# Two-layer encoder trunk on one core: weight sums and every second low part of the up weights by adding DMAs, down-projection operands made one block earlier

## The chip, the cores and the metric

The kernel runs on one core of a Trainium2 chip. The metric is the device time of one execution in microseconds (us). The kernel before was run three times; one further execution was profiled, and all rows below come from that one.

## The reference

Two layers; in each a mixer (layer 0: latent attention and stick-breaking attention side by side; layer 1: forgetting attention), a layer norm, a SwiGLU feed-forward block, a second layer norm, and a gated embedding. Everything is float32, with SEQ = 512, D_MODEL = 1024, D_FF = 2816. The change touches the feed-forward block and the loading of weights for it and for the gate:

```python
def swiglu(x, w1, w3, w2):
    return (jax.nn.silu(x @ w1) * (x @ w3)) @ w2

    for i in range(DEPTH):
        j = i // 2
        ...
        x = layer_norm(DEEPNORM_ALPHA * x + mix, ln1_g[i], ln1_b[i])
        x = layer_norm(DEEPNORM_ALPHA * x + swiglu(x, ffn_w1[i], ffn_w3[i], ffn_w2[i]), ln2_g[i], ln2_b[i])
        x = x + jax.nn.sigmoid(x @ ple_w_gate[i] + ple_b_gate[i]) * (p[i] @ ple_w_proj[i])
```

## The kernel before

Float32 products are made of three matmuls on rounded parts: each operand is split into a high part, rounded to TensorE's short float32 format, and a low part, the rest; `mm3` (L151 to L154) issues high x low, high x high and low x high. The activations stand in SBUF as x transposed, `xTh` and `xTl`. Weights come in chunks of 128 x 512 through `wload` (L138 to L149): SyncE loads `wraw` (256 KB, three buffers), ScalarE rounds it to `whi` (L147), and a subtraction makes `wlo` (L148). Which engine subtracts is told by a table; in the feed-forward block it is `DENSE`, in turn DVE, DVE, GpSimd (POOL in the profile). High and low parts have four buffers of 128 x 1024 each.

`swiglu` (L652) works on 22 blocks f of 128 hidden columns. `up` (L656) loads the pieces of w1 and w3 for one block, makes 48 matmuls into `ps_h`, and writes the gated product. The first 16 blocks are taken in four groups of four. For each group `down` (L694) makes the down-projection as seven products in place of eight (a Strassen-like scheme over halves of the hidden columns and of the output columns): `operands(m)` builds product m's activation side `bparts` (L734, L735) and its weight side, which is a block of w2 (`w2raw`, loaded as 1024 KB pieces) or a sum of such blocks, `s3` or `s1`, made by DVE and GpSimd (L713); ScalarE rounds it (L740), and DVE and GpSimd take one half each of the low part (L741). A product is 12 matmuls into `ps_m`, 84 per group. `down` is a generator, and its steps are woven into the next group's blocks, two after each `up`; `operands(m + 1)` is made ahead of product m's matmuls. The six blocks that are left (plain) follow: in the first pair of them the last group's steps are run (three, three and one), then `flush` (L767) adds up the products, and `down_pair` (L780) makes the plain blocks' own down-projection in `ps_y`. The last pair goes to `finish`, which also makes the second layer norm and the gate (L610 to L649), tile by tile of 128 rows: the statistics on ScalarE (L194), the normalising steps on DVE (L195, L199) and GpSimd (L196 to L201), the transposes of x on TensorE (`ps_xt`, L177), the gate's matmuls (`ps_g`).

The order in which instructions stand on an engine is set by a scheduler with estimates of its own, from this program order and the waits between instructions; each engine then runs its list in order. POOL's list holds GpSimd's instructions and the DMAs that GpSimd issues; all loads of weights are issued by SyncE.

## Time and profile before

| | us |
|---|---|
| three runs | 1392.1, 1392.12, 1394.07 (median 1392.12) |
| the profiled execution | 1396.08 |
| its span, first to last instruction | 1394.4 |
| mean granted TensorE clock | 0.986 of full speed |
| TensorE (PE) busy | 1346.4 (97%) |
| VectorE (DVE) busy | 925.9 (66%) |
| ScalarE (ACT) busy | 659.9 (47%) |
| GpSimd (POOL) busy | 534.1 (38%) |

The span is 1.7 us less than the execution's time; the rest lies before the first and behind the last instruction. In the rows below, L148 is line 148 of the kernel before, names are the program's tiles, out<-in, and a row of a window or group gives busy time and a count of instructions. PEclk is the granted clock as a share of full speed. "idle before, <-releaser" is the time for which an engine stood still ahead of the instruction, and the instruction that it waited for.

### The profile page before, as it was taken

To read this page: it belongs to the slowest core of one execution; us is meant where nothing else is said; L and a number is where in the kernel's file an instruction comes from. 1 tells how busy PE (TensorE), PEld (TensorE's weight loads), DVE (VectorE), ACT (ScalarE), POOL (GpSimd) and SP (SyncE) were. 2 spreads that over 40 slices of the span, in tenths; PEclk is the share of its full clock that TensorE was granted. 3 is DMA by queue.
4 is the path that set the end of the run, shared out by engine and by line. 5 is a ranking of instruction groups with operands and counts; after the bars stand their busy time and mean duration, and the time that the engine had idled before them with its cause. 6 is when DMAs were issued, how large, how long until landed. Compare 5 with 4: busy or idle time off the path is not lost.

```text
span 1394.4 us, 18865 instructions
## 1 busy us (share of the span) xinstructions
PE 1346.4 (97%) x6680; PEld 1126.1 (81%) x6680; DVE 925.9 (66%) x1600; ACT 659.9 (47%) x1362; POOL 534.1 (38%) x479
## 2 busy tenths in 40 slices
PE   7999999799999998999989999998999999989998
PEld 7888787588888887887879888876888888868887
DVE  4656778753757656948755775798346668578495
ACT  4556767552433333423455665754434334243252
POOL 5655733122334324612235554442224334255131
PEclk9999999999999999999999999999999999999999
DMA  6211321241323132232234221123413131403312
GB/s 230 89 44 47 112 66 62 90 159 61 121 83 102 58 115 89 101 105 75 73 111 131 98 91 62 61 99 105 143 56 135 54 121 44 167 32 129 98 61 98
DMA packets 64303, 131.74 MB, mean 94 GB/s; under 512 B 7361, under 2 KB 8129, under 8 KB 64193
## 3 DMA queue, kind: packets, MB, share of 16 engines
q1 hardware_dynamic: 61440, 120.74, 25.6%
q0 software_dynamic: 2768, 9.80, 2.1%
q8 instruction: 52, 0.85, 0.3%
q14 instruction: 43, 0.34, 0.1%
HBM read 127.80 MB, written 2.72 MB: 94 GB/s over the span
## 4 chain that ended last, share of the span: by engine, by line
PE 84%; DVE 9%; ACT 3%; DMA 2%; issue 2%; POOL 0%; SPq 0%; DVEq 0%; ACTq 0%; POOLq 0%
PE ps_h L154 11%; PE ps_h L153 11%; PE ps_h L152 11%; PE ps_m L152 4%; PE ps_m L153 4%; PE ps_m L154 4%; PE ps_qkT L152 3%; PE ps_qkT L153 3%; PE ps_qkT L154 3%; PE ps_y L152 2%; PE ps_o L406 2%; PE ps_y L153 2%; PE ps_y L154 2%; PE ps_g L152 2%; PE ps_g L154 2%; PE ps_g L153 2%
## 5 line engine op out<-in xcount | busy, mean ns | idle before, releaser
L148 POOL TENSOR_TENSOR wlo<-wraw,whi 128x512 fp32r<-128x512 f32 (+2 forms) x191 | 255.3, 1346 | 453.5 <-ACT whi L147 402.3
L147 ACT CAST whi<-wraw 128x512 fp32r<-128x512 f32 (+1 forms) x338 | 200.1, 616 | 323.3 <-DMA wraw<-in_ffn_w_dram 83.6
L152 PE MATMUL ps_h<-xTl,whi 128*128 128x512 f32 (+1 forms) x736 | 279.8, 380 | 0.0
L153 PE MATMUL ps_h<-xTh,whi 128*128 128x512 f32 (+1 forms) x736 | 279.6, 380 | 0.0
L154 PE MATMUL ps_h<-xTh,wlo 128*128 128x512 f32 (+1 forms) x736 | 279.5, 380 | 0.0
L148 DVE TENSOR_TENSOR wlo<-wraw,whi 128x512 fp32r<-128x512 f32 (+1 forms) x172 | 141.9, 837 | 92.9 <-ACT whi L147 90.5
L153 PEld LDWEIGHTS ps_h<-xTh,whi 128*128 128x128 f32 x736 | 138.4, 188 | 26.5
L152 PEld LDWEIGHTS ps_h<-xTl,whi 128*128 128x128 f32 x736 | 138.4, 188 | 26.2
L154 PEld LDWEIGHTS ps_h<-xTh,wlo 128*128 128x128 f32 x736 | 138.4, 188 | 26.1
L152 PE MATMUL ps_m<-wlo,bparts 128*128 128x512 f32 x224 | 89.4, 399 | 9.4 <-DVE wlo L741 8.9
L153 PE MATMUL ps_m<-whi,bparts 128*128 128x512 f32 x224 | 88.8, 396 | 0.0
L154 PE MATMUL ps_m<-whi,bparts 128*128 128x512 f32 x224 | 88.5, 395 | 0.0
L152 PE MATMUL ps_qkT<-xTl,whi 128*128 128x512 f32 x192 | 78.5, 409 | 2.4 <-DVE qkT L331 1.0
L154 PE MATMUL ps_qkT<-xTh,wlo 128*128 128x512 f32 x192 | 78.0, 406 | 0.0
L153 PE MATMUL ps_qkT<-xTh,whi 128*128 128x512 f32 x192 | 77.5, 404 | 0.0
L740 ACT CAST whi<-s 128x512 fp32r<-128x512 f32 x64 | 36.9, 619 | 85.4 <-PE ps_h L153 49.6
L741 POOL TENSOR_TENSOR wlo<-s,whi 128x512 fp32r<-128x512 f32 x32 | 42.8, 1340 | 76.3 <-ACT whi L740 76.3
L741 POOL TENSOR_TENSOR wlo<-w2raw,whi 128x512 fp32r<-128x512 f32 x24 | 34.6, 1440 | 91.9 <-ACT whi L740 83.3
L152 PE MATMUL ps_v<-wlo,xTh 128*128 128x256 f32 (+1 forms) x192 | 56.3, 294 | 6.8 <-ACT neg_tri L109 6.4
L682 DVE TENSOR_TENSOR gb<-silu,ps_h 128x256 f32<-128x256 f32 x64 | 24.0, 416 | 57.5 <-PE ps_h L154 53.7
L152 PEld LDWEIGHTS ps_m<-wlo,bparts 128*128 128x128 f32 x224 | 42.9, 192 | 20.0 <-DVE wlo L741 9.7
L210 DVE TENSOR_TENSOR x<-x,ps_y 128x512 f32<-128x512 f32 x64 | 43.0, 679 | 22.9 <-PE ps_y L154 22.6
(274 smaller groups left out, 3216.1 us busy)
## 6 DMA issues: line engine op xcount, KB each, us to landing
wraw<-in_ffn_w_dram SPq DMA_DIRECT2D x200, 256.0 KB, 2.7
w2raw<-in_ffn_w_dram SPq DMA_DIRECT2D x16, 1024.0 KB, 6.4
wraw<-in_w_gate_dram SPq DMA_DIRECT2D x32, 256.0 KB, 2.6
wraw<-in_w_qkf_dram SPq DMA_DIRECT2D x32, 256.0 KB, 2.6
wraw<-in_w_qkb_dram SPq DMA_DIRECT2D x16, 256.0 KB, 2.9
wraw<-in_a_w_out_dram SPq DMA_DIRECT2D x16, 256.0 KB, 2.6
kbias<-nd_dram POOLq DMA_DIRECT2D x8, 512.0 KB, 4.8
wraw<-in_c_w_out_dram SPq DMA_DIRECT2D x16, 256.0 KB, 2.6
```

The costliest lines, as they stand in the source:

```text
L147: (eng_hi.copy if eng_hi is acts else eng_hi.tensor_copy)(hi[:, c:end], raw)
L148: eng_lo.tensor_tensor(lo[:, c:end], raw, hi[:, c:end].bitcast(F32), ALU.subtract)
L152: nc.tensor.matmul(o, lhsT=lhs[0], rhs=rhs[1], start=first, stop=False)
L153: nc.tensor.matmul(o, lhsT=lhs[0], rhs=rhs[0], start=False, stop=False)
L154: nc.tensor.matmul(o, lhsT=lhs[1], rhs=rhs[0], start=False, stop=last)
L210: nc.vector.tensor_tensor(xs, xs, ps, ALU.add)
L406: nc.tensor.matmul(o_ps[:, kb * P:], lhsT=val[:, c:c + 2 * HD], rhs=t, start=first and n == 0, stop=last and n == 1, skip_group_check=True)
L682: nc.vector.tensor_tensor(half[:, p, k, :], s[:, fs], h[:, fs], ALU.mult)
L740: acts.copy(wh[q], ws[q])
L741: (dve, gps)[(q + m) % 2].tensor_tensor(wl[q], ws[q], wh[q].bitcast(F32), ALU.subtract)
```

## The change

Four things are changed.

**Every second low part by ScalarE and a DMA.** `SWIGLU` is the table for the weights of the feed-forward blocks, of the plain blocks' rows of w2 and of the gate's first half. One chunk in two has its low part subtracted by DVE. For the other ScalarE writes the chunk's negative into the place of `wlo`, which rounds it as the high part is rounded, and a DMA issued by GpSimd adds the chunk to it from memory once more. These are 108 chunks: 44 of w1, 44 of w3, 12 of w2's plain rows and 8 of the gate. GpSimd makes no low part of these weights any more.

**Weight sums by DMA.** `s3` and `s1` are no longer added by DVE and GpSimd from `w2raw`. Each is written by one DMA of 512 KB from w2 and then added to by another, `add` in `down`; later steps add two more blocks to `s1`. These are 48 DMAs, 16 that write and 32 that add, on GpSimd's queue. One quarter of w2 is then no longer loaded to `w2raw`. All low parts of the products' weights (L741 before) are made by DVE.

**Operands ahead.** `operands(0)` of a group is made when `down` is first entered, right behind the group's fourth block, and not with the first product's matmuls. The order of the first two products is swapped, and so are the indices of the halves.

**The plain blocks.** The last group's seven products are spread two per block over the first plain blocks, `flush` comes after the fourth of them, and both `down_pair`s of the first four stand behind the last two blocks.

The number of TensorE's matmuls, their shapes and what is computed stay as they were. The core of the diff:

```diff
...
     STICK = (acts, dve), (gps,)
     MLA = (acts, dve), (gps,)
     FOX = (acts,), (gps,)
+    SWIGLU = (acts,), (dve, nc.sync)
     engines, count = [DENSE], [0]
 
     def wload(src, n, m):
...
             count[0] += 1
             eng_hi, eng_lo = (v[count[0] % len(v)] for v in engines[0])
             (eng_hi.copy if eng_hi is acts else eng_hi.tensor_copy)(hi[:, c:end], raw)
-            eng_lo.tensor_tensor(lo[:, c:end], raw, hi[:, c:end].bitcast(F32), ALU.subtract)
+            if eng_lo is nc.sync:
+                nc.scalar.mul(lo[:, c:end], raw, -1.0)
+                gps.dma_start(lo[:, c:end], src[:, c:end], accum_op=ALU.add)
+            else:
+                eng_lo.tensor_tensor(lo[:, c:end], raw, hi[:, c:end].bitcast(F32), ALU.subtract)
         return [t[:, 0:n * m].rearrange("p (n m) -> p n m", n=n) for t in (hi, lo)]
 
     def mm3(o, lhs, rhs, first, last):
...
 
     def swiglu(i, finish):
         w1, w3, w2 = a["ffn_w1"][i], a["ffn_w3"][i], a["ffn_w2"][i]
+        engines[0] = SWIGLU
         nf = DFF // P
 
         def up(f, g, cuts=1):
...
 
 
             first = f0 == 0
+            blocks = w2[f0 * P:(f0 + 4) * P, :].rearrange("(k q p) (j c) -> p q k j c", q=2, k=2, j=2)
             raw = []
             for p in range(2):
                 t = quad("w2raw", F32)
-                nc.sync.dma_start(t.rearrange("p (k j) c -> p k (j c)", k=2),
-                                  w2[(f0 + 2 * p) * P:(f0 + 2 * p + 2) * P, :].rearrange("(k p) c -> p k c", k=2))
+                nc.sync.dma_start(t[:, 0, :], blocks[:, p, 0, 0, :])
+                nc.sync.dma_start(t[:, 2:4, :], blocks[:, p, 1])
                 raw.append(t)
             B = [[halves[i][:, :, k, :] for i in range(2)] for k in range(2)]
 
             def W(j, k):
                 return [t[:, 2 * k + j, :] for t in raw]
 
-            s3, s1 = ([wide(n)[:, q * S:(q + 1) * S] for q in range(2)] for n in ("s3", "s1"))
+            wsum = [wide(n)[:, 0:D].rearrange("p (q c) -> p q c", q=2) for n in ("s3", "s1")]
+            s3, s1 = ([t[:, q, :] for q in range(2)] for t in wsum)
+
+            def add(t, k, j, first=False):
+                gps.dma_start(t, blocks[:, :, k, j, :], accum_op=ALU.bypass if first else ALU.add)
+
+            add(wsum[0], 0, 0, True)
+            add(wsum[0], 0, 1)
+            add(wsum[1], 0, 1, True)
+            add(wsum[1], 1, 1)
             n1, n2, n3, n4 = (temp(n).rearrange("p (q s) -> p q s", q=2) for n in ("n1", "n2", "n3", "n4"))
-
-            def add(o, a, b, eng):
-                for q in range(2):
-                    eng[q].tensor_tensor(o[q], a[q], b[q], ALU.add)
 
             def operands(m):
                 tt = dve.tensor_tensor
-                ws, bs = [(W(0, 1), B[1][0]), (W(0, 0), B[0][0]), (s3, n3), (s1, n1), (s1, n2), (W(1, 1), n4),
+                ws, bs = [(W(0, 0), B[0][0]), (W(0, 1), B[1][0]), (s3, n3), (s1, n1), (s1, n2), (W(1, 1), n4),
                           (s1, B[1][1])][m]
                 if m == 2:
-                    add(s3, W(0, 0), W(1, 0), (dve, gps))
                     tt(n3, B[0][1], B[1][1], ALU.subtract)
                 elif m == 3:
-                    add(s1, W(1, 0), W(1, 1), (dve, gps))
                     tt(n1, B[0][0], B[0][1], ALU.subtract)
                 elif m == 4:
-                    add(s1, s1, W(0, 0), (dve, gps))
                     dve.scalar_tensor_tensor(n2, B[1][1], -1.0, n1, ALU.mult, ALU.subtract)
                 elif m == 5:
                     tt(n4, n2, B[1][0], ALU.add)
-                elif m == 6:
-                    add(s1, s1, W(0, 1), (dve, gps))
                 parts = act.tile([P, 2, S], F32R, tag="g", bufs=3, name="bparts")
                 bh, bl = (parts[:, c, :].rearrange("p (q s) -> p q s", q=2) for c in range(2))
                 acts.copy(bh, bs)
...
                 wh, wl = ([v[:, q * S:(q + 1) * S] for q in range(2)] for v in (hi, lo))
                 for q in range(2):
                     acts.copy(wh[q], ws[q])
-                    (dve, gps)[(q + m) % 2].tensor_tensor(wl[q], ws[q], wh[q].bitcast(F32), ALU.subtract)
+                    dve.tensor_tensor(wl[q], ws[q], wh[q].bitcast(F32), ALU.subtract)
+                if m == 3:
+                    add(wsum[1], 0, 0)
+                elif m == 4:
+                    add(wsum[1], 1, 0)
                 return (bh, bl), (wh, wl)
 
             ready = operands(0)
+            yield
             for m in range(7):
                 (bs, ws), ready = ready, operands(m + 1) if m < 6 else None
                 for tb in range(2):
                     ps = (ps_pq, ps_o)[tb]("ps_m")
                     for q in range(2):
                         mm3(ps, both(bs, lambda v: v[:, q, blk(tb)]), both(ws, lambda v: v[q]), q == 0, q == 1)
-                    if m in (0, 5, 6):
+                    if m in (1, 5, 6):
                         o = x[tb + 2 * (m == 6)][:, (m == 5) * S:(m == 5) * S + S]
                         if first:
                             dve.scalar_tensor_tensor(o, o, ALPHA, ps, ALU.mult, ALU.add)
...
 
         def flush():
 
-            q1, q7, p5, p6 = (sums[m] for m in (1, 2, 3, 4))
+            q1, q7, p5, p6 = (sums[m] for m in (0, 2, 3, 4))
             h00, h01, h10, h11 = (x_rows[:, 2 * i:2 * i + 2, j * S:(j + 1) * S] for j in range(2) for i in range(2))
             dve.tensor_tensor(p6, q1, p6, ALU.add)
             gps.tensor_tensor(h00, h00, q1, ALU.add)
...
         for f0 in range(0, 4 * GROUPS, 4):
             halves = [spare("gb").rearrange("p (q k s) -> p q k s", q=2, k=2) for _ in range(2)]
             for n in range(4):
-                up(f0 + n, as_block(halves, n // 2, n % 2), 2 if f0 + n == 0 else 1)
+                up(f0 + n, as_block(halves, n % 2, n // 2), 2 if f0 + n == 0 else 1)
                 after_up(2)
             after_up(7)
             steps = down(f0, halves)
-        waiting = None
-        for f in range(nf - plain, nf, 2):
-            group = quad("gT")
-            gs = [(group[:, 2 * j, :], group[:, 2 * j + 1, :]) for j in range(2)]
-            for j in range(2):
-                up(f + j, as_parts(gs[j]))
-                if f == nf - plain:
-                    after_up(3)
-            if waiting is None:
+            next(steps)
+        waiting = []
+        for f in range(nf - plain, nf):
+            if len(waiting) < 2:
+                g = spare("gT", F32R).rearrange("p (c s) -> p c s", c=2)
+            elif f % 2 == 0:
+                group = quad("gT")
+            if len(waiting) >= 2:
+                g = group[:, 2 * (f % 2):2 * (f % 2) + 2]
+            up(f, as_parts((g[:, 0, :], g[:, 1, :])))
+            waiting.append((g[:, 0, :], g[:, 1, :]))
+            after_up(2)
+            if f == nf - plain + 3:
                 after_up(7)
                 flush()
-            else:
-                down_pair(*waiting)
-            waiting = (f, gs)
+            if f >= nf - 2:
+                n = 2 * (f - nf + 2)
+                down_pair(nf - plain + n, waiting[n:n + 2])
+        gs = waiting[-2:]
         finish(gs, row_weights(w2, [nf - 2, nf - 1]))
 
 
...
 
         def finish(gs, w):
             first_half, rest = gate(i, e, a["w_gate"][i], done)
+            engines[0] = DENSE
             finish_rows(gs, w, False, norm_params("ln2_g", "ln2_b"), after=first_half)
             rest()
```

How the change moves instructions is shown at three places. The lines of the changed kernel are its own, five more than before from L152 on (L148 is L153, L741 is L748, L713's sums are the DMAs of L719).

POOL, layer 0, from the first group's products on: the stream of GpSimd. Before (`s_3752`, `s_3753`, `s_3754` are the weight sums of group one):

```order
L713 TENSOR_TENSOR s_3752<-w2raw 128x512
L148 TENSOR_TENSOR wlo<-wraw,whi 128x512 x5
L741 TENSOR_TENSOR wlo<-w2raw,whi 128x512 x2
L741 TENSOR_TENSOR wlo<-s_3752,whi 128x512
L713 TENSOR_TENSOR s_3754<-w2raw 128x512
L148 TENSOR_TENSOR wlo<-wraw,whi 128x512
L741 TENSOR_TENSOR wlo<-s_3753,whi 128x512
L713 TENSOR_TENSOR s_3754<-s_3754,w2raw 128x512
L741 TENSOR_TENSOR wlo<-s_3754,whi 128x512
L713 TENSOR_TENSOR s_3754<-s_3754,w2raw 128x512
L148 TENSOR_TENSOR wlo<-wraw,whi 128x512 x2
L741 TENSOR_TENSOR wlo<-w2raw,whi 128x512
```

In the changed kernel (`s_4192`, `s_4193`, `s_4695` and their like are the same sums, each DMA row one that writes and one that adds, or two that add):

```order
L151 DMA wlo<-in_ffn_w_dram 128x512 x8
L719 DMA s_4192<-in_ffn_w_dram 128x2x512 x2
L151 DMA wlo<-in_ffn_w_dram 128x512 x2
L719 DMA s_3686<-in_ffn_w_dram 128x2x512 x2
L151 DMA wlo<-in_ffn_w_dram 128x512 x2
L719 DMA s_4193<-in_ffn_w_dram 128x2x512 x2
L151 DMA wlo<-in_ffn_w_dram 128x512 x4
L719 DMA s_4695<-in_ffn_w_dram 128x2x512 x2
L151 DMA wlo<-in_ffn_w_dram 128x512 x2
L719 DMA s_4193<-in_ffn_w_dram 128x2x512 x2
```

Sums and subtractions have become DMAs, and in the steady part nothing but DMAs stands on POOL; the two DMAs of a sum stand directly ahead of the two lows of a block, and behind one another.

DVE, layer 0, at the last group: the lows of its products and what stands between them. `gT<-silu` ends a plain block. Before:

```order
L673 TENSOR_TENSOR silu<-silu,ps_h 128x512
L125 TENSOR_TENSOR gT<-silu,gT 128x512
L713 TENSOR_TENSOR s_5246<-w2raw 128x512
L741 TENSOR_TENSOR wlo<-w2raw,whi 128x512
L741 TENSOR_TENSOR wlo<-s_5246,whi 128x512
L713 TENSOR_TENSOR s_5248<-w2raw 128x512
L741 TENSOR_TENSOR wlo<-w2raw,whi 128x512
L713 TENSOR_TENSOR s_5248<-s_5248,w2raw 128x512
L764 TENSOR_TENSOR acc<-acc,ps_m 128x512 x2
L756 TENSOR_TENSOR x<-x,ps_m 128x512
```

In the changed kernel:

```order
L748 TENSOR_TENSOR wlo<-w2raw,whi 128x512 x2
L732 TENSOR_TENSOR n_5206<-gb 128x512
L748 TENSOR_TENSOR wlo<-s_5198,whi 128x512 x2
L742 TENSOR_TENSOR bparts<-n_5206,bparts 128x512
L679 TENSOR_TENSOR silu<-silu,ps_h 128x512
L153 TENSOR_TENSOR wlo<-wraw,whi 128x512
L776 TENSOR_TENSOR acc<-acc,ps_m 128x512
L125 TENSOR_TENSOR gT<-silu,gT 128x512
L776 TENSOR_TENSOR acc<-acc,ps_m 128x512
L153 TENSOR_TENSOR wlo<-wraw,whi 128x512
L768 TENSOR_TENSOR x<-x,ps_m 128x512 x2
L748 TENSOR_TENSOR wlo<-s_5199,whi 128x512 x2
```

Before, the lows of the first products come behind the first plain block's end, with sums between them. Now the first three products' lows stand ahead of that block's end, and the lows of the fourth behind it.

PE, layer 0, second layer norm: the last matmuls of the plain blocks (`ps_y`) and the first transposes of x (`ps_xt`), with buffer numbers. Before:

```order
L153 MATMUL ps_y_5979<-whi_5921,gT_5525 128x512
L154 MATMUL ps_y_5979<-whi_5921,gT_5525 128x512
L177 MATMUL ps_xt_6185<-identr_69,x_78 128x128 x4
L177 MATMUL ps_xt_6192<-identr_69,x_78 128x128 x4
L152 MATMUL ps_y_5987<-wlo_5912,gT_5525 128x512
L153 MATMUL ps_y_5987<-whi_5911,gT_5525 128x512
L154 MATMUL ps_y_5987<-whi_5911,gT_5525 128x512
```

In the changed kernel:

```order
L158 MATMUL ps_y_6180<-whi_6047,gT_5709 128x512
L159 MATMUL ps_y_6180<-whi_6047,gT_5709 128x512
L182 MATMUL ps_xt_6232<-identr_69,x_78 128x128 x4
L182 MATMUL ps_xt_6239<-identr_69,x_78 128x128 x4
L157 MATMUL ps_g_6246<-wlo_6061,xTh_76 128x512
L158 MATMUL ps_g_6246<-whi_6060,xTh_76 128x512
L159 MATMUL ps_g_6246<-whi_6060,xTl_77 128x512
```

Before, matmuls of `ps_y` stand on both sides of the transposes; now all of them stand ahead, and behind the transposes follows the gate, `ps_g`, which reads `xTh`. On ACT at the same place, before:

```order
L194 ACTIVATE ln,ss<-x,neg_mean 128x1024
L200 ACTIVATE x<-ln,rstd 128x256
L194 ACTIVATE ln,ss<-x,neg_mean 128x1024
L200 ACTIVATE x<-ln,rstd 128x256
L124 CAST xTh<-ps_xt 128x4x128 x2
L147 CAST whi<-wraw 128x512 x3
L124 CAST xTh<-ps_xt 128x4x128 x2
L147 CAST whi<-wraw 128x512 x3
L194 ACTIVATE ln,ss<-x,neg_mean 128x1024
L147 CAST whi<-wraw 128x512
```

In the changed kernel (L199 is L194, L205 is L200, L148 is L147; L150 is the multiplication by -1):

```order
L199 ACTIVATE ln,ss<-x,neg_mean 128x1024
L150 ACTIVATE wlo<-wraw 128x512
L148 CAST whi<-wraw 128x512 x3
L205 ACTIVATE x<-ln,rstd 128x256
L199 ACTIVATE ln,ss<-x,neg_mean 128x1024
L148 CAST whi<-wraw 128x512
L150 ACTIVATE wlo<-wraw 128x512
L124 CAST xTh<-ps_xt 128x4x128 x2
L148 CAST whi<-wraw 128x512
L205 ACTIVATE x<-ln,rstd 128x256
L148 CAST whi<-wraw 128x512
```

The first copies of `xTh` stand behind the second tile's statistics (`ln`) as before, but now a rounding, and multiplications with their DMAs on POOL, stand between them.

## Rows read from the trace of the kernel before

**Rows 1.** The page's first part: busy time of each engine.

```profile
PE 1346.4 (97%) x6680; PEld 1126.1 (81%) x6680; DVE 925.9 (66%) x1600; ACT 659.9 (47%) x1362; POOL 534.1 (38%) x479
```

**Rows 2.** Windows, one group, layer 0: PE, PEld, DVE, ACT, POOL busy (count), clock, DMA.

```profile
352.55:415.12 62.57, 62.57 (x278) 51.81 (x277) 39.20 (x48) 27.22 (x49) 22.26 (x16) 1.00 0.28 98
```

**Rows 3.** PE's waits over the whole span: total us, times, longest.

```profile
PE ps_m L152 <- DVE wlo L741: 8.9, 2, 4.4
```

**Rows 4.** Windows: end of the groups, both layers, and undisturbed stretches of equal length.

```profile
536.00:550.00 14.00, 9.57 (x32) 7.22 (x32) 11.28 (x12) 6.82 (x13) 9.47 (x7) 0.76 0.00 1
...
400.00:414.00 14.00, 14.00 (x63) 11.58 (x63) 10.33 (x12) 4.43 (x8) 6.02 (x5) 1.00 0.00 0
...
541.00:544.00 3.00, 3.00 (x7) 2.38 (x8) 2.97 (x2) 0.00 (x0) 2.64 (x2) 0.50 0.00 0
...
1226.00:1245.00 19.00, 14.04 (x54) 10.73 (x53) 15.96 (x17) 8.27 (x15) 12.51 (x8) 0.91 0.08 28
...
400.00:419.00 19.00, 19.00 (x85) 15.73 (x85) 13.97 (x17) 6.74 (x12) 7.94 (x7) 1.00 0.12 41
```

**Rows 5.** Timeline at the end of layer 0's groups: start us, us, instruction, idle before.

```profile
540.75 1.75 DVE L741 TENSOR_TENSOR wlo<-s,whi 128x512 fp32r<-128x512 f32 x1
...
540.88 0.80 PE L152 MATMUL ps_m<-wlo,bparts 128*128 128x512 f32 x1 [4.43 <-DVE wlo L741]
```

**Rows 6.** Timeline of the first layer norm of layer 0.

```profile
270.56 1.26 POOL L148 TENSOR_TENSOR wlo<-wraw,whi 128x512 fp32r<-128x512 f32 x1
...
270.84 1.80 DVE L199 SCALAR_TENSOR_TENSOR x<-ln,rstd,ln_b 128x768 f32<-128x768 f32 x1
```

**Rows 7.** Windows: second layer norm with the gate, both layers.

```profile
637.00:665.00 28.00, 26.72 (x130) 21.93 (x129) 25.93 (x42) 14.35 (x26) 10.14 (x13) 1.00 0.23 74
...
1327.00:1356.00 29.00, 28.08 (x136) 23.04 (x135) 27.25 (x45) 15.35 (x27) 10.99 (x14) 1.00 0.22 73
```

**Rows 8.** Timeline of that layer norm, layer 0.

```profile
638.95 1.16 ACT L194 ACTIVATE ln<-x,neg_mean 128x1024 f32<-128x1024 f32 x1 [9.04 <-DVE neg_mean L193]
...
638.95 1.28 DVE L195 SCALAR_TENSOR_TENSOR ln<-x,neg_mean,ln_g 128x1024 f32<-128x1024 f32 x1
...
640.24 0.69 DVE L210 TENSOR_TENSOR x<-x,ps_y 128x512 f32<-128x512 f32 x1
...
642.05 1.24 DVE L199 SCALAR_TENSOR_TENSOR x<-ln,rstd,ln_b 128x768 f32<-128x768 f32 x1
...
645.48 1.03 PE L177 MATMUL ps_xt<-identr,x 128*128 128x128 f32 x8
...
646.35 1.05 ACT L124 CAST xTh<-ps_xt 128x512 fp32r<-128x512 f32 x2
...
651.34 0.39 PE L152 MATMUL ps_g<-wlo,xTh 128*128 128x512 f32 x1
```

**Rows 9.** Groups by line: busy us, mean ns, idle before.

```profile
L148 POOL TENSOR_TENSOR wlo<-wraw,whi 128x512 fp32r<-128x512 f32 (+2 forms) x191 | 255.3, 1346 | 453.5 <-ACT whi L147 402.3 <-PE ps_qkT L154 9.3 <-DVE whi L147 8.0
...
L147 ACT CAST whi<-wraw 128x512 fp32r<-128x512 f32 (+1 forms) x338 | 200.1, 616 | 323.3 <-DMA wraw<-in_ffn_w_dram 83.6 <-PE ps_h L153 73.1 <-issue 65.8
...
L148 DVE TENSOR_TENSOR wlo<-wraw,whi 128x512 fp32r<-128x512 f32 (+1 forms) x172 | 141.9, 837 | 92.9 <-ACT whi L147 90.5 <-POOL wlo L148 1.5
...
L713 DVE TENSOR_TENSOR s<-w2raw 128x512 f32<-128x512 f32 x16 | 24.0, 1501 | 0.4
```

**Rows 10.** DMA issues: KB each, us from issue to landing.

```profile
wraw<-in_ffn_w_dram SPq DMA_DIRECT2D x200, 256.0 KB, 2.7
...
w2raw<-in_ffn_w_dram SPq DMA_DIRECT2D x16, 1024.0 KB, 6.4
...
kbias<-nd_dram POOLq DMA_DIRECT2D x8, 512.0 KB, 4.8
```

**Rows 11.** The tile ln_g: what one issue takes on POOL.

```profile
L182 POOL DMA_DIRECT2D ln_g<-in_ln_g_dram x4: 567/578/612, 242.7 to 1195.3; - x4
```

**Rows 12.** DMA queues: MB, share of 16 engines' span.

```profile
q1 hardware_dynamic: 61440, 120.74, 25.6%
```

## The prediction, made before the changed kernel was run

> **What bounds the kernel now.** I read the page's first part, then windows over stages, then PE's waits, then the timeline where PE waited. TensorE is busy for 97% of the span, and no other engine for more than 66% [rows 1]. The feed-forward groups, which most of this change concerns, are TensorE-bound: in the 62.57 us of one group PE is busy for all of it at full clock, with DVE at 39, ACT at 27 and POOL at 22 us [rows 2]. A group is 4 x 48 + 84 = 276 matmuls, so a matmul costs 0.227 us, and nothing that is taken from DVE or POOL in there can shorten it. What can be gained lies where PE stands idle. The longest wait in the feed-forward part is for the first low part of the last group, 4.4 us once per layer [rows 3]. The clock makes it dearer. In the 14 us from 536 on there are 32 matmuls where an undisturbed stretch of the same length has 63, and in layer 1's 19 us there are 54 against 85 [rows 4]: 31 lost per layer, 31 x 0.227 = 7.0 us. Of these 4.4 are the wait, and the rest is the half clock (0.50) that was granted behind it [rows 4]. The timeline shows why PE waited: DVE's subtractions take 1.75 us there, beside POOL's, and the first product starts as the second of them comes through [rows 5].
>
> **The change, part by part.** The sum is made against the profiled execution, 1396.08 us, with a span of 1394.4. It is 4 us above the median of the runs shown, 1392.12; I apply the differences to the median.
>
> *End of the groups.* Product 0's operands are now made as soon as the fourth block is through, and the last group's products go out two per plain block, as in the other groups, where PE never waits. Its DVE queue has blocks of lows with a block's work between (second order pair of the change). I take both stalls whole: -14.0, with -10 as the weak end if PE still waits 2 us per layer.
>
> *POOL and DVE.* 72 weight subtractions of 1346 ns on POOL and 36 of 837 ns on DVE go, and so do 32 sums of 1501 ns on DVE with POOL's own [rows 9]. In their place ScalarE gets 108 multiplications, which I price like the rounding, 616 ns [rows 9], 67 us in all, and POOL 156 issues of 0.57 to 0.61 us [rows 11], 92 us. All of this lies beside a busy PE in the groups, where ACT is busy for 27 of 62.57 us [rows 2]: nothing for the sum. Without that cover only the two layer norms are left, below.
>
> *The adding DMAs.* The trace has none, so I bound what they cost. At best one is like a plain load, 2.7 us for 256 KB; the nearest row for one that moves two operands of 512 KB is the load of 1024 KB, 6.4 us; as a dear end I take four times kbias's 4.8 us for 512 KB, 19 us [rows 10]. I take 6.4 for 512 KB and some 3.5 for 256 KB, since nothing excludes either end. POOL's queue is in order (first order pair): a sum's first DMA, then its adding DMA, which waits for the first to land, then the lows of the next block. The tightest place comes three times per layer. The last product's lows free the sum's tile 8.5 us after a block starts on PE, by DVE's place in the order. The first DMA lands at about 8.5 + 4.2 = 12.7, the adding one is issued there, and the low behind it at 13.4. It lands near 17 if it is undisturbed, and near 20 if the 512 KB ahead of it has to go through first. It is wanted 96 matmuls after the start, 96 x 0.227 = 21.8. So 2 us of slack are left, and the price is nothing. For the engines' capacity: 120.74 MB are 25.6% of 1394.4 us [rows 12], 2.96 us per MB. Per group the share of 0.28 [rows 2] is 17.5 us, and 4.2 MB of adds put 12.4 us on it for each time that their bytes count; the 62.57 us are full at about 3.6. The kernel as a whole reads some 49 MB more.
>
> The Trainium skill, "Collectives: The Full Stack", Part 3, "Why ReduceScatter is half of AllGather", says that an adding transfer needs two source reads and so runs at half a copy's rate. By that rule the 512 KB add costs about what the 1024 KB row costs, and the slack holds; no run here has shown it so far.
>
> *First layer norm.* POOL's subtraction of 1.26 us becomes an issue of 0.6, and DVE's normalising step, which took 1.80 us beside it [rows 6] and 1.24 elsewhere [rows 8], loses its neighbour. Two multiplications come onto ScalarE. About -0.8 per layer, -1.6 in all (0 to -4).
>
> *Second layer norm and gate.* Here the change costs. Before, the lows of the last two feed-forward rows came late enough that the first transposes ran between ps_y matmuls and the gate followed 12.4 us after the first statistics (638.95 to 651.34) without a gap [rows 8], with PE idle for 1.3 and 0.9 us in the stretch [rows 7]. Now all ps_y matmuls stand ahead of the first transposes (third order pair) and are through some 5 us after that point, L. ScalarE's order puts the second tile's statistics ahead of the first copy of x transposed. DVE reaches that tile's mean by five of its steps, 1.28 + 0.69 + 2 x 0.69 + 1.24, a low of 0.69 and 0.3 for the short ones: L + 5.6. ScalarE then needs 1.16 + 0.2 for the statistics, 0.62 for a rounding, 0.62 for a new multiplication and 1.05 / 2 for the copy: L + 8.7 [rows 8, 9]. The transposes end at L + 6.1, so PE waits 2.6. The gate's first half takes every second low through POOL's queue, where each is behind a tile's norm: the second is issued at L + 8.2 and lands 3.5 later, the third at L + 11.6 and lands at L + 15.1. PE wants them at 11.5 and 13.6: 0.2 and 1.5 more. That is 4.3 against 1.1, +3.2 per layer, and as at the groups' end I let the granted clock fall behind it for part of what it did there, +1.5: +4.7, or +9.4 for both. Ends: 0 if other work fills the gap, +16 if the clock is halved for the whole stretch.
>
> *Row weights of the plain blocks.* Their lows are issued a block ahead, under 96 matmuls, 21.8 us: nothing; +4 if that cover is gone.
>
> **Sum:** -14.0 - 1.6 + 9.4 = -6.2, so 1392.12 - 6.2 = 1386.
>
> **The rivals.** (a) PE does not wait at the second layer norm, since the transposed copy comes as early as before. For it: DVE's and ScalarE's steps get shorter without POOL reading beside them. Against it: the order of ScalarE. The time is 1392.1 - 15.6 = 1376.5, with up to 3 for what remains: 1378.
>
> (b) The gate's lows and the clock take all of it back: +16 for +9.4, 1392.7, no change.
>
> (c) Slower: the adding DMAs hold POOL's queue. The place is the tight one above. The point from which it decides is an add of 512 KB that takes over about 9 us, or an issue that takes over about 1.5 us on POOL. Then the next block's low is late, PE waits in the groups, and the clock falls behind it. At four times a plain one the low's own 256 KB take 4 x 2.7 = 10.8 us from 13.4 on: it lands at 24 to 25, and PE is 3 us late at six places in two layers, 18 us, and with as much again for the clock 36; with the lost layer norm of the forecast that gives 1392.1 - 6.2 + 18 to 36, 1404 to 1422. For it: PE has no slack elsewhere, and every second low of every block now hangs on this queue. Against it: POOL's queue carried 512 KB in 4.8 us [rows 10], and the engines are at 0.28.
>
> The issue of a DMA took 0.57 us on POOL at four places, where DVE was mostly idle [rows 11]. The Trainium skill, "SBUF — State Buffer", in its warning on the "DVE blocks DMA" trap, says that GpSimd cannot write descriptors while DVE holds the ports that they share. By that rule DVE's load in the groups would stretch the issues and lead to (c); no run here shows it so far.
>
> (d) The stall only moves: with all 14 lows per group on DVE, the last group's products wait elsewhere, and PE loses about the 7 us as before: 1392.1 - 7 + 7.8 = 1393, no change.
>
> **How the numbers follow.** About 0.2% (2.8 us) is what can be told from no change: 1389.3 to 1394.9. The forecast has 0.36, (a) 0.17, (b) and (d) together 0.17, (c) 0.30. Of the forecast's own range, 1381 to 1391, a fifth lies within the band. Faster: 0.29 + 0.17 = 0.46; same: 0.07 + 0.13 = 0.20; slower: 0.30 + 0.04 = 0.34. The range runs from 1377, which takes in (a), to 1412, which leaves out the dear half of (c).
>
> **What would show it.** Right: in the changed kernel's windows, 63 matmuls in 14 us around the last group with clock 1.00; in PE's waits nothing for ps_m; 2 to 3 us for ps_g behind the transposed copy, and a shorter one behind a gate low by DMA, once per layer each; adds landing within 7 us for 512 KB. Wrong: PE waiting for a DMA-made low of ps_h anywhere in the groups, adds that take over 9 us, or issues that take over 1.5 us on POOL.

## The result and the profile after

The prediction, 1386 us and faster, was wrong. The changed kernel took 1433.67 us (median of four runs, 1433.39 to 1439.72) against 1392.11 before: a ratio of 1.0306, 95% interval 1.0277 to 1.0335. It lies outside the range of the forecast, and above the 1404 to 1422 of rival (c), which had the direction and the place. The profiled execution has a span of 1438.0 us; the page's first part:

```profile
PE 1358.3 (94%) x6680; PEld 1127.4 (78%) x6680; DVE 824.9 (57%) x1588; ACT 711.3 (49%) x1470; POOL 446.2 (31%) x475
```

The other engines did get lighter, DVE by 101 us and POOL by 88 us [rows 1], and the kernel is 42 us slower. By TensorE's timelines, from marks that both kernels pass:

| us, after minus before | layer 0 | layer 1 |
|---|---|---|
| up to the first `ps_h` | +1.8 | -0.4 |
| first five blocks | 0.0 | 0.0 |
| from the first `ps_m` to the last product of the third group | +16.8 | +16.7 |
| from there to the last `ps_y` | -2.1 | -4.4 |
| from there to the last `ps_g` | +7.7 | +7.4 |

They add up to 43.5, and to the 43.6 between the spans but for rounding. The last two rows have 2.1 us per layer that only moved: 16 transposes that stood ahead of the last `ps_y` before now stand behind it.

So the loss is in the groups, where before PE had no idle moment [rows 2]. Windows over the changed kernel: two long stretches over the groups, a moment of them, the time behind a wait, and the start of the last group's products in both layers. Columns as in [rows 2]: busy times and counts of PE, PEld, DVE, ACT, POOL; granted clock; DMA share; GB/s.

```profile
300.00:536.00 236.00, 225.39 (x996) 184.19 (x996) 99.71 (x169) 97.69 (x178) 44.03 (x47) 0.99 0.65 157
990.00:1226.00 236.00, 224.53 (x1019) 185.32 (x1020) 103.38 (x176) 101.55 (x186) 47.22 (x53) 0.98 0.63 151
372.00:376.00 4.00, 4.00 (x19) 3.30 (x18) 0.00 (x0) 0.69 (x2) 0.00 (x0) 1.00 0.98 203
400.00:404.00 4.00, 4.00 (x12) 3.11 (x11) 0.69 (x1) 2.15 (x4) 0.00 (x0) 0.59 0.02 6
548.00:562.00 14.00, 14.00 (x64) 11.58 (x63) 8.07 (x13) 7.25 (x13) 2.28 (x3) 1.00 0.31 79
1260.00:1274.00 14.00, 14.00 (x63) 11.62 (x62) 7.79 (x12) 7.19 (x13) 2.02 (x3) 1.00 0.31 77
```

The last two lines answer to the first of [rows 4]. The first product of the last group, which was late by 4.4 us before, now starts at 554.96 and at 1267.23, and around it stand 64 and 63 matmuls in 14 us at clock 1.00, with no wait for `ps_m` in the whole span: the stall at the end of the groups is gone. The first line has PE idle for 10.6 us, and the share of the DMA engines is 0.65 where it was 0.28 [rows 2]; for moments it is 0.98. PE's waits over the span (total us, times, longest):

```profile
PE ps_h L159 <- DMA wlo<-in_ffn_w_dram: 26.9, 18, 3.1
PE ps_g L157 <- ACT xTh L124: 5.0, 2, 2.6
PE ps_y L157 <- DMA wlo<-in_ffn_w_dram: 4.1, 4, 1.5
PE ps_g L157 <- DMA wlo<-in_w_gate_dram: 3.4, 2, 2.1
```

18 times, nine per layer (eight in the groups, one in the plain blocks), PE waits in a block for a low part of w1 that a DMA makes, and behind four of them the granted clock falls to half for 3.4 us (0.59 from 400 to 404). The DMA view of the changed kernel: GpSimd's queue (packets, MB, share of 16 engines' span), and issues (KB each, median us to landing):

```profile
q0 software_dynamic: 29328, 63.29, 22.7%
...
wraw<-in_ffn_w_dram SPq DMA_DIRECT2D x200, 256.0 KB, 3.9
wlo<-in_ffn_w_dram POOLq DMA_DIRECT2D x100, 256.0 KB, 5.7
s<-in_ffn_w_dram POOLq DMA_DIRECT2D x48, 512.0 KB, 6.4
```

A sum's DMA lands in 6.4 us, the figure that I had for an adding one; but that is the median of 16 DMAs that only write, 4.0, and 32 that add, 7.5 (5.7 to 9.5). A low part lands in 5.7, where I had 3.5; and the plain loads of `wraw` in 3.9 for 2.7 [rows 10]. The longest of the waits in layer 0, on its timeline:

```profile
382.07 0.74 POOL L719 DMA_DIRECT2D s<-in_ffn_w_dram  x1 [4.46 <-DVE wlo L748]
388.57 1.19 POOL L719 DMA_DIRECT2D s<-in_ffn_w_dram  x1 [5.76 <-DMA s<-in_ffn_w_dram]
389.32 1.34 POOL L151 DMA_DIRECT2D wlo<-in_ffn_w_dram  x1
391.70 0.84 POOL L151 DMA_DIRECT2D wlo<-in_ffn_w_dram  x1 [1.04 <-ACT wlo L150]
...
398.47 0.50 PE L159 MATMUL ps_h<-xTh,wlo 128*128 128x512 f32 x1 [3.09 <-DMA wlo<-in_ffn_w_dram]
```

The sum's first DMA lands 6.2 us after its issue, the adding one goes out 6.5 us after it, the block's first low part right behind that, and it lands 9.1 us after its own issue, 2.0 us behind the adding DMA. The same order, a sum's adding DMA and within 2 us behind it the block's first low part, stands ahead of each of the 18 waits, and the low part landed 7 to 11 us after its issue. In eight of them it was a later addition to `s1`, with no first DMA for which the queue stood still. There are 20 such pairs of an adding DMA and a low part in all; in each the low part landed behind the addition, by 1.6 to 3.8 us.

### The profile page after: what moved, and what is told of

It reads as the page before. It is cut to its first block, busy times and chain, and to the rows that moved or that the text cites. A ratio compares the mean times of both kernels' runs of the same rounds, so it can differ in the third digit from the quotient of the medians.

```text
span 1438.0 us, 19020 instructions
## 1 busy us (share of the span) xinstructions
PE 1358.3 (94%) x6680; PEld 1127.4 (78%) x6680; DVE 824.9 (57%) x1588; ACT 711.3 (49%) x1470; POOL 446.2 (31%) x475
## 3 DMA queue, kind: packets, MB, share of 16 engines
q0 software_dynamic: 29328, 63.29, 22.7%
## 5 line engine op out<-in xcount | busy, mean ns | idle before, releaser
L148 ACT CAST whi<-wraw 128x512 fp32r<-128x512 f32 (+1 forms) x338 | 199.8, 615 | 344.5 <-issue 138.4
L159 PE MATMUL ps_h<-xTh,wlo 128*128 128x512 f32 (+1 forms) x736 | 283.8, 387 | 27.0 <-DMA wlo<-in_ffn_w_dram 26.9
L158 PE MATMUL ps_h<-xTh,whi 128*128 128x512 f32 (+1 forms) x736 | 282.7, 384 | 0.0
L153 POOL TENSOR_TENSOR wlo<-wraw,whi 128x512 fp32r<-128x512 f32 (+2 forms) x119 | 153.9, 1307 | 181.8 <-ACT whi L148 142.8
L151 POOL DMA_DIRECT2D wlo<-in_ffn_w_dram x100 | 91.9, 923 | 358.6 <-ACT wlo L150 329.9
L153 DVE TENSOR_TENSOR wlo<-wraw,whi 128x512 fp32r<-128x512 f32 (+1 forms) x136 | 105.6, 779 | 115.8 <-ACT whi L148 115.7
L719 POOL DMA_DIRECT2D s<-in_ffn_w_dram x48 | 50.5, 1052 | 233.3 <-DVE wlo L748 148.7
L748 DVE TENSOR_TENSOR wlo<-s,whi 128x512 fp32r<-128x512 f32 x64 | 46.3, 757 | 102.5 <-ACT whi L747 102.4
L158 PE MATMUL ps_m<-whi,bparts 128*128 128x512 f32 x224 | 87.1, 389 | 0.0
L159 PE MATMUL ps_m<-whi,bparts 128*128 128x512 f32 x224 | 86.2, 389 | 0.0
L150 ACT ACTIVATE wlo<-wraw 128x512 fp32r<-128x512 f32 x108 | 67.6, 626 | 0.0
```

The source lines that it names most:

```text
L148: (eng_hi.copy if eng_hi is acts else eng_hi.tensor_copy)(hi[:, c:end], raw)
L150: nc.scalar.mul(lo[:, c:end], raw, -1.0)
L151: gps.dma_start(lo[:, c:end], src[:, c:end], accum_op=ALU.add)
L153: eng_lo.tensor_tensor(lo[:, c:end], raw, hi[:, c:end].bitcast(F32), ALU.subtract)
L158: nc.tensor.matmul(o, lhsT=lhs[0], rhs=rhs[0], start=False, stop=False)
L159: nc.tensor.matmul(o, lhsT=lhs[1], rhs=rhs[0], start=False, stop=last)
```

## The experiments

Three theories stood after this. **A**: adding transfers hold the DMA engines about twice as long as a copy, and low parts land late for that load. **B**: GpSimd's queue, in order, holds the low part back while it waits for a sum's first DMA. **E**, formed later: a low part has to wait until the 512 KB of the adding DMA ahead of it are through.

**The order alone**, and **each use of the adding DMAs alone.** `order_only` is the changed kernel with

```diff
-    SWIGLU = (acts,), (dve, nc.sync)
+    SWIGLU = DENSE
...
-                    dve.tensor_tensor(wl[q], ws[q], wh[q].bitcast(F32), ALU.subtract)
+                    (dve, gps)[(q + m) % 2].tensor_tensor(wl[q], ws[q], wh[q].bitcast(F32), ALU.subtract)
```

and `add` as before the change (sums by DVE and GpSimd, w2 loaded whole). `lows_engines` has the first of these edits alone, `sums_engines` the old `add` alone.

> The changed program order alone: operands of a group made ahead, the last group's products spread over the plain blocks; all low parts and all weight sums are made by the engines as in the kernel before, and no DMA adds. If the order does what the prediction said, the wait of 4.4 us and the half clock behind it go in both layers and nothing else comes: 1392 - 14 = 1378, 1376 to 1382. Rival: the order only moves the stall (with DVE and GpSimd still adding the sums, the products' operands come late elsewhere): 1388 or more, with a wait of ps_m for a low part.

> The changed kernel with the low parts of the up weights, of the plain rows and of the gate made by DVE, DVE and GpSimd in turn; the weight sums stay with the adding DMAs. Theory A (the adding low parts load the DMA engines twice per byte, and land late) and theory B (the low part's DMA stands on GpSimd's queue behind a sum's) both take PE's waits for low parts away: about 1380, 1376 to 1388. Rival C: the sums by DMA are late for ScalarE, which rounds them in the same list as the up weights' chunks; then PE waits go on, 1395 or more.

> The changed kernel with the weight sums made by DVE and GpSimd from w2raw, as before; every second low part stays with an adding DMA. Theory B (the low part waits on GpSimd's queue behind a sum's first DMA and the one that adds to it): PE's waits for low parts go, and only the second layer norm's loss stays: about 1390, 1385 to 1396. Theory A (the DMA engines): 25 MB of sums leave the engines and 4 MB of w2 come back, the adding low parts stay; about half of PE's waits stay: 1405 to 1420.

| | us, median | ratio to before, 95% interval |
|---|---|---|
| order_only | 1378.42 | 0.9898 (0.9884 to 0.9913) |
| lows_engines | 1380.88 | 0.9916 (0.9894 to 0.9939) |
| sums_engines | 1395.99 | 1.0021 (1.0011 to 1.0030) |

The order is worth the 14 us that were forecast for it: 7.0 per layer between the third group and the last `ps_y` by the timelines, and nothing lost in the groups. All three are within a range that was given for them, but `sums_engines` is within B's, and outside the 1405 to 1420 of A, which had half of the waits stay. Either use of the adding DMAs alone leaves the groups without a wait for a low part; `lows_engines` has one of 0.3 us for `bparts` and loses 0.9 us there. The same window as above, `sums_engines`, then its low parts:

```profile
300.00:536.00 236.00, 236.00 (x1055) 195.87 (x1054) 125.56 (x196) 106.59 (x194) 45.35 (x44) 1.00 0.49 125
```

```profile
wlo<-in_ffn_w_dram POOLq DMA_DIRECT2D x100, 256.0 KB, 5.1
```

What `sums_engines` loses to `order_only`, 17.6 us, lies at the plain rows and the second layer norm by the timelines. Sums alone cost 2.5 us and low parts alone 17.6, but both together 55.3: some 35 us come from their meeting in the groups.

**Copies for adding DMAs, with every engine's list unchanged.** The addition is left out of the low parts, of the sums, or of both:

```diff
-                gps.dma_start(lo[:, c:end], src[:, c:end], accum_op=ALU.add)
+                gps.dma_start(lo[:, c:end], src[:, c:end], accum_op=ALU.bypass)
...
-                gps.dma_start(t, blocks[:, :, k, j, :], accum_op=ALU.bypass if first else ALU.add)
+                gps.dma_start(t, blocks[:, :, k, j, :], accum_op=ALU.bypass)
```

> The changed kernel with each of the 108 adding low-part DMAs replaced by a plain copy of the same bytes on the same queue; what is left out is the addition, so these low parts hold the raw weights. Every engine's list is the same. Theory A (an adding transfer holds the DMA engines about twice as long as a copy): low parts land in about 4 us for 5.7, the DMA share in the groups falls from 0.65 to about 0.53, and more than half of PE's waits go: 1400 to 1412. Theory B (the order of the queue): landing falls a little, the waits stay: 1425 to 1434.

> The changed kernel with the 32 adding DMAs of the weight sums replaced by plain copies of the same bytes on the same queue; what is left out is the addition, so s3 and s1 hold one block of w2 each. Every engine's list is the same, the low parts still add. Theory A (engine time of the adding DMAs): replacing 28.3 MB of low parts gave 30 us; 16.8 MB of sums should give about 30 x 16.8 / 28.3 = 18: 1416, 1410 to 1421. Theory B (the low part held on GpSimd's queue by a sum's DMAs, whose issue waits for the DMA before it and for DVE): the waits of the issues stay as they are, 1428 to 1434.

> Both replacements together: all 140 adding DMAs become copies of the same bytes; the additions of the sums and of the low parts are left out. Every engine's list is the same as in the changed kernel. Theory A: the DMA share in the groups falls to about 0.5, as in the two kernels with one kind of adding DMA alone, whose groups had no wait; then the groups have none or little, and what is left over the kernel with the order alone (1378) is the second layer norm and the plain rows, 16 to 18 us less a little: 1390 to 1397. Theory B: the order of the queue still makes the waits that were left when the low parts were copies: 1400 or more, waits for low parts of 8 us or more in the groups.

| | us, median | ratio to before, 95% interval |
|---|---|---|
| lows_copy | 1403.40 | 1.0082 (1.0061 to 1.0102) |
| sums_copy | 1410.68 | 1.0136 (1.0119 to 1.0154) |
| both_copy | 1385.94 | 0.9955 (0.9940 to 0.9970) |

The first two are within A's ranges, the third is 4 us below its own. `both_copy`, the two windows, and its DMA view:

```profile
300.00:536.00 236.00, 236.00 (x1052) 195.85 (x1052) 109.48 (x185) 105.55 (x192) 29.82 (x49) 1.00 0.50 160
990.00:1226.00 236.00, 236.00 (x1043) 195.46 (x1042) 111.78 (x188) 104.95 (x191) 30.66 (x51) 1.00 0.51 161
```

```profile
q0 software_dynamic: 25232, 63.29, 14.9%
...
wlo<-in_ffn_w_dram POOLq DMA_DIRECT2D x100, 256.0 KB, 4.1
s<-in_ffn_w_dram POOLq DMA_DIRECT2D x48, 512.0 KB, 4.4
```

With the same lists, the same bytes and the same waits on GpSimd's queue the groups have no wait, and 48 us are gone. Theory B falls; it had 1400 or more. It is the additions. Their engine time: 22.7% of 1438.0 us less 14.9% of 1384.0 is 120 us for 45.1 MB, 2.7 us per MB on top of a copy's 206 us / 63.29 MB = 3.3, so 1.8 times a copy. The Trainium skill, "Collectives: The Full Stack", Part 3, "Why ReduceScatter is half of AllGather", says of the add in a reduce step that it needs two source reads and so runs at half a copy's rate; the 1.8 here is near that.

**Is it the engines' load, or what stands ahead of the low part?** Into `both_copy` a plain store of 256 KB is put beside each low part, issued by ScalarE on its own queue (`load1`, one; `load2`, two):

```diff
+                for _ in range(1):
+                    nc.scalar.dma_start(dram.tile([P, S], F32, name="load"), hi[:, c:end].bitcast(F32))
```

> The kernel in which all adding DMAs are copies (1386), with a plain store of 256 KB put beside each of the 108 low parts: the same chunk's high part goes to a scratch area in memory that nobody reads, issued by ScalarE, so GpSimd's queue and the low parts' own DMAs are as they were. The additions are left out as there. 28 MB of plain transfers take about the engine time that the 28.3 MB of adding low parts took beyond a copy. Theory A (engine time alone): waits for low parts in the groups come back, 1398 to 1412. Rival D (the adding DMA's own issue on GpSimd, 0.9 us for 0.55, and its own later landing): none come back, 1386 to 1390, beside what 108 issues cost ScalarE.

> The same with two such stores per low part, 57 MB, more engine time than all additions took together (about 130 us of the 16 engines). Theory A: the groups wait as in the changed kernel or more, 1425 to 1450. Rival D: 1386 to 1392.

They took 1393.75 us (1.0000, 0.9990 to 1.0011) and 1416.12 us (1.0147, 1.0107 to 1.0186): `load1` short of what A expected, `load2` short of it too, and neither D's. The lists moved in places in these two, so they do not compare as strictly as the copies. The window and the low parts' landing, `load1`:

```profile
300.00:536.00 236.00, 235.63 (x1059) 195.60 (x1058) 106.12 (x181) 104.33 (x190) 29.83 (x49) 1.00 0.62 198
```

```profile
wlo<-in_ffn_w_dram POOLq DMA_DIRECT2D x100, 256.0 KB, 4.6
```

and `load2`, with its wait on PE:

```profile
300.00:536.00 236.00, 233.02 (x1035) 191.84 (x1034) 105.15 (x180) 104.53 (x190) 29.87 (x49) 1.00 0.71 230
```

```profile
wlo<-in_ffn_w_dram POOLq DMA_DIRECT2D x100, 256.0 KB, 5.7
```

```profile
PE ps_h L161 <- DMA wlo<-in_ffn_w_dram: 13.3, 9, 5.3
```

`load1` has a DMA share of 0.62, the same as `sums_copy` (0.62 and 0.60, with 8.0 us of such waits), and one short wait of 0.4 in layer 0's groups. At 0.71 the waits do come, but of the 13.3 us the longest, 5.3, and another of 0.9 lie in the plain blocks; the groups have 7.1, where the changed kernel has 22.8 of its 26.9 at 0.65. Load on another queue makes low parts late, but it takes more of it than of additions on their own queue. So A is a part, not the whole.

**The adding DMA ahead of the low part.** `adds_small` leaves the sums' first DMAs at 512 KB and cuts what is added to 32 of 512 columns:

```diff
-                gps.dma_start(t, blocks[:, :, k, j, :], accum_op=ALU.bypass if first else ALU.add)
+                if first:
+                    gps.dma_start(t, blocks[:, :, k, j, :])
+                else:
+                    gps.dma_start(t[:, :, 0:32], blocks[:, :, k, j, 0:32], accum_op=ALU.add)
```

> The changed kernel with the sums' adding DMAs cut from 512 columns of a block to 32 (16 KB per half for 256 KB); what is left out is the rest of the sums. The sums' first DMAs move 512 KB as before, and the adding ones still wait for them on GpSimd's queue; the low parts still add. In the changed kernel all 18 low parts for which TensorE waited in the groups were issued right behind a sum's adding DMA and landed 7 to 9 us after their issue. Theory E (a low part behind a sum's adding DMA has to wait until its 512 KB are through): they now land in about 5 us as with the sums on the engines, and the groups have no wait or little: 1396 to 1402, where the kernel with sums by the engines had 1396. Theory B (GpSimd's queue waits for the first DMA): the waits of 2 to 3 us, once per group, stay: 1408 to 1420.

1398.84 us (1.0032, 1.0017 to 1.0046). Its window, its low parts, and the waits of the sums' issues on POOL:

```profile
300.00:536.00 236.00, 235.55 (x1054) 195.35 (x1054) 108.08 (x182) 105.06 (x191) 45.74 (x49) 1.00 0.57 136
```

```profile
wlo<-in_ffn_w_dram POOLq DMA_DIRECT2D x100, 256.0 KB, 5.3
```

```profile
POOL s L722 <- DMA s<-in_ffn_w_dram: 48.7, 15, 4.5
```

POOL still stands 48.7 us for the sums' first DMAs (56.1 in the changed kernel), the low parts still add, at 5.3 us, and the groups are all but free of waits. That is what E expected, in its range of 1396 to 1402. This kernel also has less load (0.57) and lists that moved in places. But `lows_copy`, whose low parts are copies and stand behind whole additions, has the same load and still waits, 12.1 us in all:

```profile
300.00:536.00 236.00, 230.84 (x1035) 190.42 (x1034) 104.59 (x178) 102.65 (x186) 35.91 (x49) 1.00 0.58 163
```

So it is what stands ahead of the low part, more than the mean load. Whether it is held up in the order of one queue's transfers, or by the engines that both need at once, is not shown outright; the packets in the traces lean to the order. In `both_copy` a sum's packets have 4096 bytes and a low part's 2048. A low part with nothing ahead of it on the queue starts to move 1.3 to 2.3 us after its issue, one issued up to 1.1 us behind a sum's DMA after 2.2 to 3.5 us, and in all 19 pairs at least 80 of the sum's 128 packets had started by then. With adding DMAs both have 2048 bytes, and the packets can't be told apart.

**The second layer norm and the plain rows.** `gate_engines` is the changed kernel with `engines[0] = DENSE` one line higher, ahead of the gate's first half; `lows_up_only` has the old `add`, and `SWIGLU` set for the pieces of w1 and w3 alone:

```diff
+            engines[0] = SWIGLU
             pieces = [wload(w[f], KT, P) for w in (w1, w3)]
+            engines[0] = DENSE
```

> The changed kernel with the gate's first half taken off the adding DMAs: its low parts by DVE, DVE and GpSimd in turn. If the gate's DMA-made low parts and their multiplications on ScalarE make the loss at the second layer norm (+5.7 per layer in the trace), 1433.7 - 8 to 12 = 1422 to 1426. Rival: the loss comes from the order of TensorE's list, all ps_y ahead of the transposes, which the plain rows' low parts set: then only the waits for the gate's low parts go, 1433.7 - 3 to 5 = 1429 to 1431.

> Weight sums by the engines; adding DMAs for every second low part of w1 and w3 alone, those of the plain rows and of the gate by the engines; order of the program as changed. The kernel with sums by the engines lost 17.6 us to the one with the order alone, in its trace 2 per layer at the plain rows and 6.8 at the second layer norm, none in the groups. If that is so, this one has none of it: 1378 to 1381. Rival: the adding DMAs in the groups cost at the layer norms or at the plain blocks as well: 1384 or more.

`gate_engines`: 1427.27 us (1.0239, 1.0210 to 1.0268), 6.4 less than the changed kernel and between the two expectations. The waits for the gate's low parts are gone, and those for `xTh` are smaller but still there (2.8 us in all for 5.0), which fits a part that TensorE's order costs; no run changes that order alone. `lows_up_only`: 1375.79 us (0.9879, 0.9865 to 0.9894). It is 2 us under its range, loses none of the 17.6 us, and with every second low part of w1 and w3 still made by an adding DMA its groups have no wait:

```profile
300.00:536.00 236.00, 236.00 (x1050) 195.74 (x1050) 128.03 (x198) 105.58 (x193) 46.69 (x44) 1.00 0.48 126
```

It is the fastest kernel of the study, 17 us below the one before and 58 below the changed one; against `order_only` the intervals of the two overlap.

## Why the prediction was wrong

*The end of the groups: right.* -14.0 forecast, 1378.42 with the order alone. The stall did not move, so rival (d) is out.

*The adding DMAs: the step that failed,* and with it the answer. It said that "2 us of slack are left, and the price is nothing". The mean load was about right: the group's 17.5 us and twice the 12.4 us for the additions are 0.68 of 62.57 us, and 0.65 was measured. An addition of 512 KB was priced a little low, 6.4 us for a median of 7.5. Wrong was what lies between issues and landings at the tight place. From the start of the block ahead (372.38 on PE's timeline) the sum's first DMA was issued after 9.7 us where I had 8.5; the adding one went out 6.5 later for 4.2, beside 1.5 MB of w2 that SyncE loads at that moment; and the low part landed 9.1 us after its issue where I had 3.5 to 6.6. It landed 26.1 us after that start, where I had 17 to 20: three errors of one sign used up the slack, and PE waited 3.1 us. I had taken each duration from rows in which the engines were at 0.28, and put it into a stretch where they stand at 0.78 and then at 0.95:

```profile
382.00:391.00 9.00, 9.00 (x42) 7.44 (x41) 5.13 (x9) 5.00 (x10) 2.84 (x3) 1.00 0.78 272
391.00:398.40 7.40, 4.38 (x20) 3.30 (x18) 1.29 (x2) 1.44 (x3) 0.84 (x1) 1.00 0.95 186
```

I also looked at three such places per layer; there are ten low parts right behind a sum's adding DMA, and TensorE waits for nine of them. Eight waits per layer in the groups make 10.5 and 12.4 us by the timelines, and the half clock behind some of them costs 3.4 us in layer 0 (two stretches of 3.4 us at 0.50) and 1.7 in layer 1 (one). With about 0.3 us around each wait, in the spacing of the matmuls, that is nearly all of the 16.8 and 16.7 us of the table's third row.

*Rival (c)* had the place, TensorE's wait for a low part behind a sum, and the time, 1404 to 1422, too low. Its points of decision, an add of over 9 us or an issue of over 1.5, were not needed: one of 32 adds took over 9 us, and no issue over 1.4; the medians are 0.86 us for a low part and 1.19 for a sum. The groups by line (busy us, mean ns of one):

```profile
L151 POOL DMA_DIRECT2D wlo<-in_ffn_w_dram x100 | 91.9, 923 | 358.6 <-ACT wlo L150 329.9
...
L719 POOL DMA_DIRECT2D s<-in_ffn_w_dram x48 | 50.5, 1052 | 233.3 <-DVE wlo L748 148.7
```

I had 0.57 to 0.61 [rows 11]. The longer issue was not needed for the waits: in `lows_copy` a low part's issue takes 0.54 us (median), and 12.1 us of them are left. What the Trainium skill's "SBUF — State Buffer" warns of with the "DVE blocks DMA" trap, which I had put behind (c), did not show: no issue of a low part or a sum took over 1.4 us, with DVE busy for 42% of the groups. But the warning is worded for DVE operations in a two-port mode, such as a float32 copy, and DVE's work in the groups is mostly `TENSOR_TENSOR` subtractions and products, so this case hardly tests it. The prediction also misread its rows there: DVE was busy through two of the four issues of [rows 11] (0.59 and 0.61 us) and idle through the other two (0.57).

*The second layer norm: right, and undersized.* The chain came as worked out. PE waits 2.4 us for the copy of `xTh`, where I had 2.6:

```profile
667.95 1.03 PE L182 MATMUL ps_xt<-identr,x 128*128 128x128 f32 x8
...
670.75 1.05 ACT L124 CAST xTh<-ps_xt 128x512 fp32r<-128x512 f32 x2
...
671.37 0.50 PE L157 MATMUL ps_g<-wlo,xTh 128*128 128x512 f32 x1 [2.39 <-ACT xTh L124]
```

and then 2.1 for a gate low part (1.3 in layer 1), where I had 0.2 and 1.5. With the transposes that moved taken off, the stage costs 5.7 us in layer 0 and 5.3 in layer 1, against 4.7.

*The plain rows: wrong.* Priced at nothing "under 96 matmuls"; PE waits 4.1 us for four of their low parts. `sums_engines` shows it without the groups' trouble, 2 us per layer. In the changed kernel the stretch from the third group to the last `ps_y` loses 7.0 and 4.7 us against `order_only`, with the transposes reckoned in: the wait for a low part of w1 in each layer's plain blocks (2.2 and 1.8 us) and, in layer 0, a half clock behind it lie there too.

*The first layer norm:* -0.8 per layer forecast, +1.8 and -0.4 measured. In layer 0 the first group's sums stand ahead of `ln_g` and `ln_b` on POOL's queue, which I did not count as a move past that queue. `ln_g` goes out 0.7 us behind an adding DMA, lands 8.4 us after its issue, and DVE waits for it:

```profile
272.43 1.28 DVE L200 SCALAR_TENSOR_TENSOR ln<-x,neg_mean,ln_g 128x1024 f32<-128x1024 f32 x1 [4.99 <-DMA ln_g<-in_ln_g_dram]
```

With the sums on the engines (`order_only`, `sums_engines`) the same stage is 2.4 and 2.3 us shorter than before; with adding DMAs for the sums alone (`lows_engines`) it is 0.8 longer, and with copies for all (`both_copy`) 2.8 shorter.

Taken together, the sum was right for transfers that cost what copies cost: `both_copy`, the changed kernel without its additions, takes 1385.94 us for the 1386 of the forecast. That the terms for the layer norms and the plain rows were each off by a few us is hidden in that figure.

## What to carry to other kernels

Work handed to a DMA queue is hidden only while the queue's landings are on time where they meet: price a transfer with the load and with the transfer ahead of it at that place, not with its median elsewhere, and let no small late-needed transfer follow a large adding one on the same queue. Two such moves that alone cost the groups nothing, or under 1 us, can cost 35 us together. And where a change has several parts, the part that pays may be the one that moves no work: here the order of the products.

## What the runs showed of the hardware that I had not expected

- An adding DMA's issue is longer on GpSimd than a copy's of the same shape: 0.86 us median for 0.54 (256 KB, the changed kernel and `lows_copy`).
- Load from another queue, 28 MB more at a DMA share of 0.62, left low parts of 256 KB on time (4.6 us), while a 512 KB addition ahead on their own queue made them land 7 to 11 us after their issue at a share of 0.65.
- Plain loads on SyncE's queue slow down with the load on the other queues: `wraw` 2.7 us before, 3.5 with low parts adding alone, 2.9 with sums alone, 3.9 with both, 3.3 with both as copies, 4.2 in `load1`.
